# Prompt attention on one Trainium2 core: a third bank for the transposes, a factor chain in two parts, and low halves subtracted on VectorE

## The chip, the cores and the metric

The program runs on one core of a Trainium2 chip, as one launch. The metric is the device time in microseconds of that core. The kernel before took 2014.07 us in the median of three runs (2012.44, 2014.07 and 2017.64). The engines are TensorE (PE for its matmuls, PEld for its weight loads), VectorE (DVE), ScalarE (ACT), GpSimd (POOL) and SyncE (SP, which issues most DMAs). Each engine works through its own queue in order.

## The reference, cut to what matters

One inference step of a two-layer decoder trunk, for a prompt of 1024 tokens and for 8 samples of 8 tokens. Layer 0 is a gated short convolution beside a memory cross-attention. Layer 1 is a latent attention with 8 heads beside a memory cross-attention. The change touches the prompt's latent attention in layer 1:

```python
q  = (rms_norm(cq, q_lora_g) @ w_uq).reshape(b, t, 8, 192)   # 128 plain + 64 rotary per head
qn = rms_norm(q, q_g)                                        # a factor per row and head
k_nope = einsum('btc,chd->bthd', ckv, w_uk)
kscale = rsqrt((sum(k_nope**2) + sum(kpe_raw**2)) / 192 + EPS)   # a factor per key and head
s = (q_abs . ckv + q_pe . kpe) * kscale * 192**-0.5          # causal, rows of 128 queries
p = softmax(s);  o_lat = p @ ckv
y_mla = einsum('bthc,chd->bthd', o_lat, w_uv)
out = concat(y_mla, y_mem) * silu(z);  y = x + out @ w_out
```

The kernel computes keys, queries and values per head from the latent (k = ckv w_uk, v = ckv w_uv), so that s = q k and y = p v directly.

## The kernel before, in words

All matrix products are made of fp32 numbers split into a high half (fp32r) and a low half (the rest), and are three matmuls each: high by high, low by high, high by low (helper `mm3`, lines 188 to 191). A split is two instructions: the high half is a copy that rounds, the low half a subtraction (helpers `sub`, line 179, and `split`, lines 181 to 186). Most rows of the profile that say L179 or L183 are such a subtraction or copy; the names of the tiles tell which. Weights come through the class `Stream`, which loads a tile, and splits it with the engines named in its arguments `le` (the low half; `"g"` is GpSimd, `"v"` VectorE) and `he` (the high half).

The program runs a long first part (both layers' projections and the samples' attention), then the preparation of the prompt's attention (`mla_pre`), then `mla()`, which is the eight heads, and then `out1()`, the last projection. In `mla()`, head h is worked on while head h+1 is prepared:

- `prep(h)` is a generator. It makes the head's keys (tiles `akH`, `akL`) and queries (`aqH`, `aqL`) with matmuls into the PSUM banks called `mm` (three of them), and the squares `asq`; then the sums of squares through the bank `v` (`ast`), and from these the factors 1/sqrt in a chain of small VectorE instructions on 128x16 numbers (`akv`, `aks`, `rsq`: lines 1376 to 1378, and `rsqrt_`, lines 202 to 206). The factors are transposed (`tk`), copied (`akt`), written to DRAM and read back as a row over all partitions (`akb`), which the scores need. Each `yield` gives way to the head that is being worked on.
- `vals(h)` makes the values of two heads at once (`avH`, `avL`), in even heads, in the steps i = 2 to 5.
- For each of eight blocks of 128 queries (i = 0 to 7): `soft` makes the scores (matmuls L1421 to L1427 into `mm` banks), multiplies them by `akb` and takes the maximum on VectorE (L1429, tile `ass`), makes the bias `anb` (L1432) and the exponentials on ScalarE (L1434), then the reciprocal `als`, and `scale` multiplies by it on ScalarE (L1441; i = 0 on VectorE). Two blocks later `step` follows: `tr` transposes the probabilities 128x128 by 128x128 into PSUM banks (`atp`, L1453), up to four to a bank; `trs` splits the bank into `aPTH` (ScalarE) and `aPTL` (VectorE); for every second i, `pvl` multiplies by the values into `aO` and VectorE multiplies by the gate (`as`, L1480).

In `prep` and `vals`, the lines `psplit(...)` split a bank of keys, queries or values. With `"g"` ScalarE copies the bank to `araw` in SBUF (L1320), GpSimd rounds it to the high half (L1321) and subtracts (L179); the bank is free after ScalarE. With `"v"` ScalarE writes the high half from the bank (L1324) and VectorE subtracts from the bank (L179, or L1328 for the queries, which carry a factor). Head 0 uses `"v"` for all; for the others the strings `PSP` (keys, queries) and `VSP` (the four parts of the values) decide. `O_ENG` names the engines for the last projection's weights (`who`, `wlo`).

The order of the instructions on each engine is set when the program is built: a scheduler takes the instructions of the generators and places each by its estimate of when it can start. PSUM has eight banks here: three `mm`, two with the tag `s` (where the transposes go), and one each with the tags `v`, `t` and `x`; `x` isn't used in `mla()`.

Of the kernel before, what the change touches and what calls it, by code (L numbers as in the profile page):

```python
# [5 lines left out]
F = mybir.dt.float32  # L6
R = mybir.dt.float32r
I32 = mybir.dt.int32
# [4 lines left out]
ALU = mybir.AluOpType  # L13
# [38 lines left out]
M_ENG = ("vvgv", "a")  # L52
A_ENG = ("v", "a")
SCL = "vaaaaaaa"
PSP = "ggg"
W_ENG = ("v", "a")
PT_ENG = "a"
NY = 7.0
MRB = 2
WQ = 1024  # L60
VSP = "vggg"
VI = (2, 3, 4, 5)
SLAG = 1
O_ENG = ("g", "a")
YG = ()
YORD = [(0, 2)] + [(b, x) for b in (11, 0, 1, 2, 3, 4, 5, 6, 7) for x in range(2)]
YLB = 6
# [25 lines left out]
def build(nc, tc, I, O):  # L93
    A, V, G, T, S = nc.scalar, nc.vector, nc.gpsimd, nc.tensor, nc.sync
# [38 lines left out]
    def mmt(name="mm"):  # L133
        return psm.tile([128, 512], F, tag="mm", name=name)

    def pst(tag, name):
        return psx.tile([128, 512], F, tag=tag, name=name, bufs=2 if tag == "s" else 1)
# [55 lines left out]
    cnt = [0]  # L193
    sm = {}

    def rsqrt_(p, out, v, shape):

        cnt[0] += 1
        t = p.tile(shape, F, tag="rsq", name=f"rsq{cnt[0]}")
        P = shape[0]  # L200
        t, out, v = t[0:P], out, v
        V.tensor_scalar(out=out.bitcast(I32), in0=v.bitcast(I32), scalar1=-0.5, scalar2=float(0x5F3759DF), op0=ALU.mult, op1=ALU.add)
        for _ in range(3):
            V.tensor_tensor(out=t, in0=out, in1=out, op=ALU.mult)
            V.scalar_tensor_tensor(out=t, in0=t, scalar=-0.5, in1=v, op0=ALU.mult, op1=ALU.mult)
            V.scalar_tensor_tensor(out=out, in0=t, scalar=1.5, in1=out, op0=ALU.add, op1=ALU.mult)

    def stat_r(p, sqs, tiles, n, tag, eps=EPS, keep=None):

        nt = len(tiles)  # L210
        ps = pst("x", "stat" + tag)
        for i, (c0, m) in enumerate(tiles):
            for j, sq in enumerate(sqs):
                T.matmul(ps[0:m, 2 * i:2 * i + 2], sq[:, c0:c0 + m], ones[:, 0:2], start=(j == 0), stop=(j == len(sqs) - 1))
        v = (keep or p).tile([128, nt], F, name="stv" + tag, tag="stv" + (tag if keep else ""))
        r = (keep or p).tile([128, nt], F, name="str" + tag, tag="str" + (tag if keep else ""))
        if tiles[-1][1] < 128:
            V.memset(v, 1.0)
        for i0, i1, m in ([(0, nt, 128)] if tiles[-1][1] == 128 else [(0, nt - 1, 128), (nt - 1, nt, tiles[-1][1])]):
            V.tensor_scalar(out=v[0:m, i0:i1], in0=ps[0:m, 2 * i0:2 * i1].rearrange("p (i two) -> p i two", two=2)[:, :, 0], scalar1=1.0 / n, scalar2=eps, op0=ALU.mult, op1=ALU.add)  # L220
        rsqrt_(p, r, v, [128, nt])
        return v, r
# [1009 lines left out]
    def mla_pre():  # L1232
# [12 lines left out]
        V.memset(fac[:, 0:8], 1.0 / 192)  # L1245
        V.scalar_tensor_tensor(out=fac[:, 8:16], in0=rcq[:, 0:8], scalar=1.0 / 192, in1=rcq[:, 0:8], op0=ALU.mult, op1=ALU.mult)
        pw = P.new("mw_")
        wq = Stream(pw, pw, [I["wuqn"][h] for h in range(8)], 384, "q", bufs=1)
        pw2 = P.new("mw2_")
        wk = Stream(pw2, pw2, [I["wuk"][h] for h in range(8)], 256, "k", bufs=1)  # L1250
        pw3 = P.new("mw3_")
        wv = Stream(pw3, pw3, [I["wuv"][h] for h in range(4)], 512, "v", bufs=1)
        wk.load_to(0)
        wq.load_to(0)
        wv.load_to(0)
# [11 lines left out]
        p = tp_.new("mt2")  # L1267
# [8 lines left out]
        p = tp_.new("mt3")  # L1276
        for i in range(8):
            ps = mmt()
# [16 lines left out]
            if i in CKI[0:2]:  # L1295
                k = CKI.index(i)
# [12 lines left out]
    def mla():  # L1309
        yield "X"  # L1310
        P, cqH, cqL, ckH, ckL, kpH, kpL, ssq, fac, wq, wk, wv = sm["mla"]
        LP = Pools()
        p = LP.new("ma_")
# [3 lines left out]
        def psplit(le, h, l, ps, scale=1.0):  # L1317
            if le == "g":
                t = p.tile([128, 512], F, name="araw", tag="araw", bufs=3)
                A.activation(t, ps, AF.Copy, scale=scale)  # L1320
                G.tensor_copy(h, t)  # L1321
                sub(G, l, t, h)
            else:
                A.activation(h, ps, AF.Copy, scale=scale)  # L1324
                if isinstance(scale, float):
                    sub(V, l, ps, h)
                else:
                    V.scalar_tensor_tensor(out=l, in0=ps, scalar=scale, in1=h.bitcast(F), op0=ALU.mult, op1=ALU.subtract)  # L1328

        def prep(h):  # L1330
# [7 lines left out]
            qp = p.tile([128, NP], R, name="aqp", tag=f"aqp{h % 2}")  # L1338
            qr = p.tile([128, NP], F, name="aqr", tag="aqr")
            S.dma_start(out=qr[0:64], in_=d_qp[h // 2, 64 * (h % 2):64 * (h % 2) + 64, :])  # L1340
            yield 0.5
            for c in range(2):
                ps = mmt()
                fm(ps, 512, w, 2, ckH, ckL, c * 512)
                sq = p.tile([128, 512], F, name="asq", tag="asq", bufs=4)
                A.activation(sq, ps, AF.Square)
                psplit("v" if h == 0 else PSP[0], kH[:, c * 512:(c + 1) * 512], kL[:, c * 512:(c + 1) * 512], ps)
                sqs.append(sq)
                if c == 0:
                    w2 = wq.get(h)  # L1350
                q = slice(c * 512, (c + 1) * 512)
# [4 lines left out]
            for c in range(2):  # L1356
                ps = mmt()
                fm(ps, 512, w, 3, cqH, cqL, c * 512)
                sq = p.tile([128, 512], F, name="asq", tag="asq", bufs=4)
                A.activation(sq, ps, AF.Square)  # L1360
                psplit("v" if h == 0 else PSP[1], qH[:, c * 512:(c + 1) * 512], qL[:, c * 512:(c + 1) * 512], ps, gq)
                sqs.append(sq)
# [11 lines left out]
            v = p.tile([128, 16], F, name="akv", tag="akv")  # L1374
            rs = p.tile([128, 16], F, name="aks", tag="aks")
            V.tensor_tensor(out=v.rearrange("p (j c) -> p j c", j=4), in0=st, in1=ssq[:, :, h].rearrange("p (j c) -> p j c", j=4), op=ALU.add)
            V.tensor_tensor(out=v, in0=v, in1=fac, op=ALU.mult)
            V.tensor_scalar(out=v, in0=v, scalar1=EPS, scalar2=None, op0=ALU.add)
            rsqrt_(p, rs, v, [128, 16])
            yield 1.0  # L1380
            tk = pst("v", "tk")
            T.transpose(tk[0:8, 0:128], rs[:, 0:8], ident)
            kt = p.tile([8, 128], F, name="akt", tag="akt")
# [58 lines left out]
            else:  # L1442
                V.tensor_scalar(out=ss[:, 0:kv], in0=ss[:, 0:kv], scalar1=ls, scalar2=None, op0=ALU.mult)

        PTs = {}

        def tr(i, ss):
            out = []
            for b0 in range(0, i + 1, 4):
                nb = min(4, i + 1 - b0)  # L1450
                ps = pst("s", "atp")
                for b in range(nb):
                    T.transpose(ps[:, b * 128:(b + 1) * 128], ss[:, (b0 + b) * 128:(b0 + b + 1) * 128], ident)  # L1453
                out.append((b0, nb, ps))
            return out
# [13 lines left out]
        def pvl(h, i, H, L):  # L1469
# [15 lines left out]
            end()  # L1485

        g0 = prep(0)
        for _ in range(5):
            next(g0)
# [14 lines left out]
        def step(h, i, ss):  # L1504
            t = tr(i, ss)
            flush()
            trs(h, i, t)
# [69 lines left out]
    def out1_pre():  # L1577
# [3 lines left out]
        pw = PR.new("o1w")  # L1581
        ws = Stream(pw, pw, [I["wo1"][u] for u in range(8)], 1536, "o1", *O_ENG, rbufs=1)
        ws.load_to(0)
# [239 lines left out]
    def chain(*gens):  # L1823
        for g in gens:
            yield from g

    fr = chain(group_a(GA, I["xA"]), ["P"], samp_prep(), ["S"], samp_attn(), samp_y(), ["Y", "pre"], mla_pre(), ["X"])
    fl = chain(mem_kv(), group_b(GB, I["xB"]), mla(), out1())
    interleave(fl, fr, RAT)
    S.dma_start(out=O["newc"], in_=newc)  # L1830
# [121 lines left out]
```

## Time and profile before

| | |
|---|---|
| median of three runs | 2014.07 us (2012.44 to 2017.64) |
| the profiled execution | 2021.16 us, of which the span of the trace is 2019.4 us |
| TensorE matmuls busy | 1918.3 us, 95% of the span |
| VectorE busy | 983.4 us, 49% |
| ScalarE busy | 744.7 us, 37% |
| GpSimd busy | 474.6 us, 24% |

The profiled execution is 7 us longer than the median of the runs. The page's shares are means over the whole program; the eight heads lie between 1560 and 1884 us, `out1()` behind them. In a row of the timeline, the number in square brackets is the time for which the engine sat idle before the instruction, and the name behind it what ended that.

### The profile page before, as it was taken

The numbers are of one execution on the slowest core, as the hardware profiler recorded it, in microseconds if no ns is written. First come the engines' busy times: TensorE is split into PE (matmuls) and PEld (weight loads), VectorE is DVE, ScalarE is ACT, GpSimd is POOL, SyncE is SP. The second block draws the span as 40 slices with busy tenths as digits, with TensorE's granted clock in tenths as the row PEclk, the third lists the DMA queues.
The fourth block names the chain that finished last, engine by engine and source line by source line (L and its number), as shares of the span: only waits on it lengthen the run. The fifth ranks groups of instructions, "written<-read, shape, count | busy, mean of one in ns | idle before, by whom it ended". The sixth has DMA issues, their size and how long they took to land. (4 is left out here: it accounts for less than half of the span.)

```text
span 2019.4 us, 35704 instructions
## 1 busy us (share of the span) xinstructions
PE 1918.3 (95%) x12508; PEld 1653.9 (82%) x12508; DVE 983.4 (49%) x2673; ACT 744.7 (37%) x1499; POOL 474.6 (24%) x493
## 2 busy tenths in 40 slices
PE   6998999999999999999999999999998899998999
PEld 5997998999997877777787766777787787787999
DVE  7659535456544434434322543444446656656300
ACT  6445223334311233323222422333333666666300
POOL 1200000000000233323433324333332443432120
PEclk8999999999999999999999989999999999999999
DMA  5563535433544688678997879877852211213532
GB/s 202 193 207 124 165 131 194 145 117 114 181 160 140 194 266 270 221 249 281 321 314 260 292 235 301 255 240 231 284 156 67 84 58 56 67 40 129 183 95 72
DMA packets 192884, 368.28 MB, mean 182 GB/s; under 512 B 27809, under 2 KB 135585, under 8 KB 191426
## 3 DMA queue, kind: packets, MB, share of 16 engines
q1 hardware_dynamic: 172178, 298.75, 45.5%
q0 software_dynamic: 20528, 67.26, 10.3%
q8 instruction: 99, 1.62, 0.3%
q14 instruction: 79, 0.65, 0.1%
HBM read 331.22 MB, written 34.70 MB: 181 GB/s over the span
## 5 line engine op out<-in xcount | busy, mean ns | idle before, releaser
L1078 POOL DMA_INDIRECT nat<-nat,IX x256 | 270.6, 1057 | 517.9 <-PE pv L1163 451.6
L189 PE MATMUL mm<-xH,whi 128*128 128x384 f32 (+1 forms) x1112 | 369.1, 332 | 6.5 <-ACT whi L183 6.5
L191 PE MATMUL mm<-xH,wli 128*128 128x384 f32 (+1 forms) x1112 | 364.0, 328 | 1.8 <-DVE wli L179 1.8
L190 PE MATMUL mm<-xL,whi 128*128 128x384 f32 (+1 forms) x1112 | 364.0, 327 | 0.0
L189 PEld LDWEIGHTS mm<-xH,whi 128*128 128x128 f32 x1112 | 211.6, 190 | 22.5 <-issue 10.0
L183 ACT ACTIVATE whi<-wri 128x1024 fp32r<-128x1024 f32 (+1 forms) x130 | 126.4, 979 | 278.2 <-PE mm L190 228.4
L190 PEld LDWEIGHTS mm<-xL,whi 128*128 128x128 f32 x1112 | 211.4, 190 | 3.0 <-issue 2.8
L191 PEld LDWEIGHTS mm<-xH,wli 128*128 128x128 f32 x1112 | 211.1, 190 | 3.3 <-DVE wli L179 2.6
L179 DVE TENSOR_TENSOR wli<-wri,whi 128x1024 fp32r<-128x1024 f32 (+1 forms) x130 | 147.0, 1136 | 123.9 <-ACT whi L183 122.6
L1163 PE MATMUL pv<-nat,PT 128*64 128x256 f32 x1024 | 141.0, 397 | 16.6 <-ACT PT L1143 13.8
L1092 PE MATMUL sAB<-rec,qar 128*64 128x256 f32 x1024 | 150.4, 389 | 1.9 <-DVE mx L1107 1.6
L1163 PEld LDWEIGHTS pv<-nat,PT 128*64 128x64 f32 x1024 | 76.6, 140 | 60.6 <-ACT PT L1143 21.3
L1092 PEld LDWEIGHTS sAB<-rec,qar 128*64 128x64 f32 x1024 | 79.4, 138 | 45.5 <-issue 12.8
L1107 DVE CUSTOM_DVE_ANT_1 ss<-sAB,rec,mx 128x256 f32<-128x256 f32 x120 | 57.9, 483 | 113.3 <-PE sAB L1097 68.8
L189 PE MATMUL mm<-nH,whi 128*128 128x384 f32 x304 | 104.8, 345 | 1.1 <-ACT mP L497 1.0
L190 PE MATMUL mm<-nL,whi 128*128 128x384 f32 x304 | 102.7, 338 | 0.1
L191 PE MATMUL mm<-nH,wli 128*128 128x384 f32 x304 | 102.2, 336 | 0.0
L189 PE MATMUL mm<-yHo,who 128*128 128x384 f32 (+1 forms) x288 | 96.9, 337 | 1.3 <-ACT yHo L183 1.3
L191 PE MATMUL mm<-yHo,wlo 128*128 128x384 f32 (+1 forms) x288 | 94.2, 327 | 0.0
L190 PE MATMUL mm<-yLo,who 128*128 128x384 f32 (+1 forms) x288 | 93.9, 326 | 0.0
L183 ACT ACTIVATE who<-wro 128x768 fp32r<-128x768 f32 (+3 forms) x44 | 38.1, 873 | 146.7 <-PE mm L190 115.5
L1434 ACT ACTIVATE ass<-ass,anb,arq 128x128 f32<-128x128 f32 (+3 forms) x64 | 55.4, 866 | 63.6 <-DVE anb L1432 63.6
(588 smaller groups left out, 4196.3 us busy)
## 6 DMA issues: line engine op xcount, KB each, us to landing
rec<-rec SPq DMA_DIRECT2D x512, 192.0 KB
wri<-wi SPq DMA_DIRECT2D x114, 512.0 KB
wro<-wo SPq DMA_DIRECT2D x29, 384.0 KB
smkv<-ckm SPq DMA_DIRECT2D x16, 512.0 KB
smkv<-cvm SPq DMA_DIRECT2D x16, 512.0 KB
wrm<-memw SPq DMA_DIRECT2D x7, 1024.0 KB
wro<-wo SPq DMA_DIRECT2D x7, 768.0 KB
yld<-d_ys SPq DMA_DIRECT2D x8, 544.0 KB
```

The costliest lines, as they stand in the source:

```text
L179: eng.tensor_tensor(out=out, in0=a, in1=h.bitcast(F), op=ALU.subtract)
L183: A.activation(h, src, AF.Copy)
L189: T.matmul(out, wh, xh, start=first, stop=False)
L190: T.matmul(out, wh, xl, start=False, stop=False)
L191: T.matmul(out, wl, xh, start=False, stop=last)
L1078: G.indirect_dma_start(out=t[:, j % 2, :], out_offset=None, in_=I["nat"], in_offset=bass.IndirectOffsetOnAxis(ap=IX[:, q:q + 1], axis=0), ...
L1092: T.matmul(s[x][64 * ab:64 * ab + 64, 0:256], QA[:, cb, b, :], part(t, cb * 128 + ab * 64)[:, 4 * x:4 * x + 4, :], start=(cb == 0), stop=F ...
L1107: V.tensor_tensor_reduce(out=ss[:, 256 * x:256 * x + 256].rearrange("p (g k) -> p g k", g=4), in0=s[x][:, 0:256].rearrange("p (g k) -> p g ...
L1163: T.matmul(d["v"][64 * ab:64 * ab + 64, 0:256], PT[:, j, ab, :], n[j][:, ab * 256:ab * 256 + 256], start=(i == 0 and j == 0), stop=(i == C ...
L1434: A.activation(ss[:, 0:kv], ss[:, 0:kv], AF.Exp, bias=nb, scale=d["rq"][:, i:i + 1], accum_out=ls)
```

## The change

```diff
--- before.py
+++ after.py
@@ -52,16 +52,16 @@
 M_ENG = ("vvgv", "a")
 A_ENG = ("v", "a")
 SCL = "vaaaaaaa"
-PSP = "ggg"
+PSP = "vvv"
 W_ENG = ("v", "a")
 PT_ENG = "a"
 NY = 7.0
 MRB = 2
 WQ = 1024
-VSP = "vggg"
+VSP = "vvvv"
 VI = (2, 3, 4, 5)
 SLAG = 1
-O_ENG = ("g", "a")
+O_ENG = ("v", "a")
 YG = ()
 YORD = [(0, 2)] + [(b, x) for b in (11, 0, 1, 2, 3, 4, 5, 6, 7) for x in range(2)]
 YLB = 6
@@ -204,6 +204,18 @@
             V.tensor_tensor(out=t, in0=out, in1=out, op=ALU.mult)
             V.scalar_tensor_tensor(out=t, in0=t, scalar=-0.5, in1=v, op0=ALU.mult, op1=ALU.mult)
             V.scalar_tensor_tensor(out=out, in0=t, scalar=1.5, in1=out, op0=ALU.add, op1=ALU.mult)
+
+    def rsqrt_steps(p, out, v, shape):
+
+        cnt[0] += 1
+        t = p.tile(shape, F, tag="rsq", name=f"rsq{cnt[0]}")
+        V.tensor_scalar(out=out.bitcast(I32), in0=v.bitcast(I32), scalar1=-0.5, scalar2=float(0x5F3759DF), op0=ALU.mult, op1=ALU.add)
+        for n in range(3):
+            V.tensor_tensor(out=t, in0=out, in1=out, op=ALU.mult)
+            V.scalar_tensor_tensor(out=t, in0=t, scalar=-0.5, in1=v, op0=ALU.mult, op1=ALU.mult)
+            V.scalar_tensor_tensor(out=out, in0=t, scalar=1.5, in1=out, op0=ALU.add, op1=ALU.mult)
+            if n != 1:
+                yield
 
     def stat_r(p, sqs, tiles, n, tag, eps=EPS, keep=None):
 
@@ -1245,11 +1257,11 @@
         V.memset(fac[:, 0:8], 1.0 / 192)
         V.scalar_tensor_tensor(out=fac[:, 8:16], in0=rcq[:, 0:8], scalar=1.0 / 192, in1=rcq[:, 0:8], op0=ALU.mult, op1=ALU.mult)
         pw = P.new("mw_")
-        wq = Stream(pw, pw, [I["wuqn"][h] for h in range(8)], 384, "q", bufs=1)
+        wq = Stream(pw, pw, [I["wuqn"][h] for h in range(8)], 384, "q", "v", bufs=1)
         pw2 = P.new("mw2_")
-        wk = Stream(pw2, pw2, [I["wuk"][h] for h in range(8)], 256, "k", bufs=1)
+        wk = Stream(pw2, pw2, [I["wuk"][h] for h in range(8)], 256, "k", "v", bufs=1)
         pw3 = P.new("mw3_")
-        wv = Stream(pw3, pw3, [I["wuv"][h] for h in range(4)], 512, "v", bufs=1)
+        wv = Stream(pw3, pw3, [I["wuv"][h] for h in range(4)], 512, "v", "v", bufs=1)
         wk.load_to(0)
         wq.load_to(0)
         wv.load_to(0)
@@ -1338,7 +1350,6 @@
             qp = p.tile([128, NP], R, name="aqp", tag=f"aqp{h % 2}")
             qr = p.tile([128, NP], F, name="aqr", tag="aqr")
             S.dma_start(out=qr[0:64], in_=d_qp[h // 2, 64 * (h % 2):64 * (h % 2) + 64, :])
-            yield 0.5
             for c in range(2):
                 ps = mmt()
                 fm(ps, 512, w, 2, ckH, ckL, c * 512)
@@ -1376,8 +1387,8 @@
             V.tensor_tensor(out=v.rearrange("p (j c) -> p j c", j=4), in0=st, in1=ssq[:, :, h].rearrange("p (j c) -> p j c", j=4), op=ALU.add)
             V.tensor_tensor(out=v, in0=v, in1=fac, op=ALU.mult)
             V.tensor_scalar(out=v, in0=v, scalar1=EPS, scalar2=None, op0=ALU.add)
-            rsqrt_(p, rs, v, [128, 16])
-            yield 1.0
+            for _ in rsqrt_steps(p, rs, v, [128, 16]):
+                yield 0.5
             tk = pst("v", "tk")
             T.transpose(tk[0:8, 0:128], rs[:, 0:8], ident)
             kt = p.tile([8, 128], F, name="akt", tag="akt")
@@ -1442,13 +1453,14 @@
             else:
                 V.tensor_scalar(out=ss[:, 0:kv], in0=ss[:, 0:kv], scalar1=ls, scalar2=None, op0=ALU.mult)
 
-        PTs = {}
+        PTs, ntr = {}, [0]
 
         def tr(i, ss):
             out = []
             for b0 in range(0, i + 1, 4):
                 nb = min(4, i + 1 - b0)
-                ps = pst("s", "atp")
+                ps = pst("ssx"[ntr[0] % 3], "atp")
+                ntr[0] += 1
                 for b in range(nb):
                     T.transpose(ps[:, b * 128:(b + 1) * 128], ss[:, (b0 + b) * 128:(b0 + b + 1) * 128], ident)
                 out.append((b0, nb, ps))
```

In the eight heads the low halves of keys, queries and values, and those of the weights of all three and of the last projection, are subtracted on VectorE; the high halves are written by ScalarE straight from the bank. GpSimd keeps the rotary half of the queries (`aqp`, two instructions a head) and small copies. The transposes go round three banks (s, s, x). The `yield` ahead of the keys is gone, so that everything in `prep` comes one step earlier, and the chain of factors is cut in two by a `yield` behind its first round.

The instructions of GpSimd that go leave it with this in the heads: two `aqp` for each head. On VectorE and TensorE the order changes as follows; line numbers of the changed kernel are 12 higher from line 217 on (L1429 becomes L1440, L1453 becomes L1465, and the chain's L202 to L206 become L212 to L216).

VectorE, where the head turns: block 0 of a head (`ass` 128x128) and what follows it, before:

```order
L1429 ISA ass,amx<-mm,akb 128x128
L1429 ISA amx 128x1
L1432 SCALAR_TENSOR_TENSOR anb<-amx,arq 128x1
L1435 RECIPROCAL als<-als 128x1
L1443 TENSOR_SCALAR ass<-ass,als 128x128
L1480 SCALAR_TENSOR_TENSOR as_21609<-as_21609,aO 128x256
L179 TENSOR_TENSOR aPTL<-atp,aPTH 128x4x128
L179 TENSOR_TENSOR aPTL<-atp,aPTH 128x3x128
L1429 ISA ass,amx<-mm,akb 128x256
L1429 ISA amx 128x1
```

and after the change, with the keys of the next head (`akL`) and a weight (`wlk`) in the same place:

```order
L1440 ISA ass,amx<-mm,akb 128x128
L1440 ISA amx 128x1
L1443 SCALAR_TENSOR_TENSOR anb<-amx,arq 128x1
L179 TENSOR_TENSOR akL<-mm,akH 128x512
L1446 RECIPROCAL als<-als 128x1
L1454 TENSOR_SCALAR ass<-ass,als 128x128
L179 TENSOR_TENSOR akL<-mm,akH 128x512
L179 TENSOR_TENSOR wlk<-wrk,whk 128x256
L1492 SCALAR_TENSOR_TENSOR as_21593<-as_21593,aO 128x256
L179 TENSOR_TENSOR aPTL<-atp,aPTH 128x4x128
L179 TENSOR_TENSOR aPTL<-atp,aPTH 128x3x128
L1440 ISA ass,amx<-mm,akb 128x256
```

The two subtractions of keys stand ahead of the `aPTL` of block 6 (the 4x128 and the 3x128).

VectorE, blocks 5 and 6 of a head, where the chain of factors (L204 to L206 on `rsq` and `aks`) meets the `aPTL` of block 3 (128x4x128), before:

```order
L205 SCALAR_TENSOR_TENSOR rsq_22046<-rsq_22046,akv 128x16
L206 SCALAR_TENSOR_TENSOR aks<-rsq_22046,aks 128x16
L204 TENSOR_TENSOR rsq_22046<-aks 128x16
L205 SCALAR_TENSOR_TENSOR rsq_22046<-rsq_22046,akv 128x16
L1429 ISA ass,amx<-mm,akb 128x512
L1429 ISA amx 128x1
L206 SCALAR_TENSOR_TENSOR aks<-rsq_22046,aks 128x16
L179 TENSOR_TENSOR aPTL<-atp,aPTH 128x4x128
L204 TENSOR_TENSOR rsq_22046<-aks 128x16
L1429 ISA ass,amx<-mm,akb,amx 128x384
L1429 ISA amx 128x1
```

and the same `aPTL` after the change, where the chain (L214 to L216) has ended ahead of it:

```order
L1443 SCALAR_TENSOR_TENSOR anb<-amx,arq 128x1
L216 SCALAR_TENSOR_TENSOR aks<-rsq_21958,aks 128x16
L214 TENSOR_TENSOR rsq_21958<-aks 128x16
L215 SCALAR_TENSOR_TENSOR rsq_21958<-rsq_21958,akv 128x16
L216 SCALAR_TENSOR_TENSOR aks<-rsq_21958,aks 128x16
L1401 SCALAR_TENSOR_TENSOR arq<-aks,rcq 128x8
L1446 RECIPROCAL als<-als 128x1
L179 TENSOR_TENSOR avL<-mm,avH 128x512
L179 TENSOR_TENSOR aPTL<-atp,aPTH 128x4x128
L1440 ISA ass,amx<-mm,akb 128x512
L1440 ISA amx 128x1
L1395 COPY akt<-tk 8x128
```

The chain begins a block of scores earlier than before; in a head with values, `avL` and `wlv` stand in between, and `anb` of block 6 behind `wlv`.

TensorE in the same head, from the transposes of block 3 (`atp` x4), before:

```order
L1453 MATMUL atp<-ident,ass 128x128 x4
L189 MATMUL aO<-aPTH,avH 128x256
L1421 MATMUL mm<-akH,aqH 128x512
L1453 MATMUL atp<-ident,ass 128x128
L190 MATMUL aO<-aPTL,avH 128x256
L191 MATMUL aO<-aPTH,avL 128x256
L189 MATMUL aO<-aPTH,avH 128x256
L190 MATMUL aO<-aPTL,avH 128x256
L191 MATMUL aO<-aPTH,avL 128x256
L189 MATMUL aO<-aPTH,avH 128x256
L1382 MATMUL tk<-ident,aks 8x128
```

and after:

```order
L1436 MATMUL mm<-kpL,aqp 128x384
L1438 LDWEIGHTS idb
L1438 MATMUL mm<-cmb,idb 128x128
L1393 MATMUL tk<-ident,aks 8x128
L1465 MATMUL atp<-ident,ass 128x128 x5
L189 MATMUL aO<-aPTH,avH 128x256
L190 MATMUL aO<-aPTL,avH 128x256
L191 MATMUL aO<-aPTH,avL 128x256
L189 MATMUL aO<-aPTH,avH 128x256
L190 MATMUL aO<-aPTL,avH 128x256
```

The transpose of the factors (`tk`) stands ahead of all transposes of block 4, which are now in one row, and no longer among the products `aO`.

## Rows read from the trace of the kernel before

**Rows 1.** Windows by stage: length, busy us (instructions) by engine, PE clock, DMA share, GB/s.

```profile
1560.00:1602.00 42.00, 38.03 (x207) 29.11 (x206) 22.60 (x68) 24.49 (x51) 17.36 (x17) 0.92 0.32 92
1602.00:1830.00 228.00, 212.05 (x1390) 179.35 (x1389) 136.19 (x447) 149.99 (x298) 92.08 (x94) 0.99 0.20 62
1830.00:1884.00 54.00, 49.50 (x317) 44.30 (x316) 35.43 (x91) 38.24 (x61) 5.85 (x6) 0.94 0.50 168
```

**Rows 2.** Waits of PE, 1602 to 1830 us: total us, times, longest.

```profile
PE atp L1453 <- DVE rsq L204: 9.9, 6, 3.0
PE atp L1453 <- DVE aPTL L179: 5.0, 6, 0.8
PE aO L189 <- ACT aPTH L183: 0.7, 3, 0.2
PE tk L1382 <- DVE aks L206: 0.3, 1, 0.3
```

**Rows 3.** Timeline, 1673 to 1678 us: start, duration, engine, line, tile, idle before.

```profile
1673.30 1.31 POOL L179 TENSOR_TENSOR avL<-araw,avH 128x512 fp32r<-128x512 f32 x1
1673.50 1.15 DVE L206 SCALAR_TENSOR_TENSOR aks<-rsq,aks 128x16 f32<-128x16 f32 x1
1674.58 1.27 POOL L179 TENSOR_TENSOR wlv<-wrv,whv 128x512 fp32r<-128x512 f32 x1
1674.68 1.20 DVE L204 TENSOR_TENSOR rsq<-aks 128x16 f32<-128x16 f32 x1
...
1676.70 0.68 DVE L179 TENSOR_TENSOR aPTL<-atp,aPTH 128x512 fp32r<-128x512 f32 x1
...
1677.53 0.45 PE L1453 MATMUL atp<-ident,ass 128*128 128x128 f32 x1 [2.37 <-DVE rsq L204]
```

**Rows 4.** Timeline of head 1, which makes no values, 1634 to 1645 us.

```profile
1634.50 0.17 DVE L206 SCALAR_TENSOR_TENSOR aks<-rsq,aks 128x16 f32<-128x16 f32 x1
...
1636.53 0.30 PE L1453 MATMUL atp<-ident,ass 128*128 128x128 f32 x1 [0.71 <-DVE rsq L204]
...
1644.55 0.55 PE L1453 MATMUL atp<-ident,ass 128*128 128x128 f32 x3 [0.84 <-DVE aPTL L179]
```

**Rows 5.** Windows of 8 us with a low clock; columns as in rows 1.

```profile
1572.00:1580.00 8.00, 4.84 (x22) 4.01 (x21) 5.02 (x10) 1.95 (x5) 3.51 (x3) 0.67 0.27 68
...
1676.00:1684.00 8.00, 6.47 (x36) 5.89 (x37) 5.90 (x22) 4.21 (x8) 0.52 (x1) 0.79 0.33 102
...
1828.00:1836.00 8.00, 6.23 (x33) 5.38 (x33) 5.82 (x21) 4.67 (x8) 2.01 (x3) 0.79 0.39 128
```

**Rows 6.** Groups on DVE: line, tile, form, count | busy us, mean ns | idle before.

```profile
L1432 DVE SCALAR_TENSOR_TENSOR anb<-amx,arq 128x1 f32<-128x1 f32 x64 | 21.0, 329 | 1.2
...
L179 DVE TENSOR_TENSOR avL<-mm,avH 128x512 fp32r<-128x512 f32 x7 | 4.8, 687 | 0.4 <-ACT avH L1324 0.3
...
L1328 DVE SCALAR_TENSOR_TENSOR aqL<-mm,gq,aqH 128x512 fp32r<-128x512 f32 x2 | 1.5, 751 | 2.8 <-ACT aqH L1324 2.8
...
L179 DVE TENSOR_TENSOR wli<-wri,whi 128x256 fp32r<-128x256 f32 x16 | 6.3, 424 | 2.4 <-ACT whi L183 2.0 <-issue 0.4
```

**Rows 7.** Group on POOL that stays, 1560 to 1884 us.

```profile
L179 POOL TENSOR_TENSOR aqp<-aqr,aqp 64x512 fp32r<-64x512 f32 x16 | 20.3, 1284 | 66.0 <-issue 60.8 <-ACT aqp L1352 5.0
```

**Rows 8.** A bank held by VectorE in head 0 (timeline); VectorE's longest wait, all heads.

```profile
1567.62 0.19 PEld L189 LDWEIGHTS mm<-whv,ckH 128*128 128x128 f32 x1 [0.84 <-DVE aqL L1328]
...
DVE als L1435 <- ACT ass L1434: 37.3, 46, 1.2
```

**Rows 9.** Timeline of head 0: the factors' transpose, and the first scores.

```profile
1576.39 0.37 PE L1382 MATMUL tk<-ident,aks 128*8 128x128 f32 x1 [2.99 <-DVE aks L206]
...
1583.28 0.29 DVE L1429 CUSTOM_DVE_ANT_0 ass<-mm,akb 128x128 f32<-128x128 f32 x1 [6.12 <-DMA akb<-d_ks]
```

**Rows 10.** Timeline of head 7: a load for the last projection, and PE behind it.

```profile
1854.50 1.11 ACT L183 ACTIVATE yHp<-yr 128x1088 fp32r<-128x1088 f32 x1 [2.87 <-DMA yr<-d_ym]
...
1857.89 1.39 PE L1453 MATMUL atp<-ident,ass 128*128 128x128 f32 x5 [2.33 <-DVE aPTL L179]
```

## The prediction

> **What bounds the kernel now.** I read the stages first, then TensorE's waits in the stage that the change touches, then the instructions around the longest waits, and last VectorE's groups there. In the windows by stage [rows 1] the reader is to see that TensorE is nearly the whole of the eight heads: in heads 1 to 6 it is busy for 212.05 of 228.00 us while VectorE is for 136.19, ScalarE for 149.99 and GpSimd for 92.08. So only TensorE's idle time can be won, and what its clock loses: 228.00 − 212.05 = 15.95 us in heads 1 to 6, 3.97 in head 0 (with the start) and 4.50 in head 7 and the step into the last projection, 24.4 in all. The clock column gives (1 − 0.92) × 42 + (1 − 0.99) × 228 + (1 − 0.94) × 54 = 3.4 + 2.3 + 3.2 = 8.9 us of full-speed time lost. The two together, 33 us, are the most that this change can save there.
>
> TensorE's waits [rows 2] are the 15.9 us of heads 1 to 6, and nearly all of it is the transposes `atp` waiting for VectorE. They wait for a bank. The six waits of 0.8 us on `aPTL` are the bank itself [rows 4]. The 9.9 us put down to the factor chain are the same thing: the transpose of block 4's last part stops until the `aPTL` of block 3 has emptied one of the two banks, and that `aPTL` stands in VectorE's queue in the middle of the chain. The trace shows it: `aPTL` runs from 1676.70 for 0.68 us, and TensorE starts again at 1677.53 after 2.37 us [rows 3]. These waits are short, 0.71 us, in heads without values [rows 4] and 2.4 to 3.0 us in heads with values. The difference is GpSimd: an instruction of the chain that takes 0.17 us by itself [rows 4] takes 1.15 us beside GpSimd's `avL` and 1.20 us beside its `wlv`, and ends when they end [rows 3].
>
> **The change part by part.** *Third bank and earlier chain.* With banks s, s, x, a transposition reuses a bank three allocations later instead of two, so that block 4's last part needs the bank of block 2, whose `aPTL` is done well before. The six waits of 0.8 us and the six on the chain's `aPTL` lose their cause: −9.9 − 5.0 − 0.3 (`tk`) = −15.2 us. What is late next: the products `aO` of blocks 2 and 3 need the `aPTL` of block 3, and this now stands behind the end of the chain and, with values, behind an `avL`. The rows show such a wait only as 0.7 us in three heads [rows 2]; at worst all of `avL` and `aPTL`, 0.69 + 0.68 = 1.4 us [rows 6, 3], is waited for in each of the six heads, 8 us. In heads with values TensorE has 12 matmuls of values and ten scores ahead of it. I take 0.5 us a head, nearer to the row that there is: +3. Six heads: 15.95 − 3 = −13 us.
>
> *GpSimd's subtractions.* On VectorE come, per the groups' durations [rows 6]: 14 `akL` and 9 `avL` at 0.687 us, 14 `aqL` at 0.751, and the weights. Between 256 and 512 columns a subtraction grows by (687 − 424)/256 = 1.03 ns a column, so 7 `wlk` at 0.424, 7 `wlq` (384 columns) at 0.556, 3 `wlv` at 0.687, and in head 7 four pieces of `wlo` at 0.556 and one of 1536 columns at 1.74: 15.8 + 10.5 + 3.0 + 3.9 + 2.1 + 4.0 = 39.3 us in the heads. What goes on VectorE is the stretching: 64 `anb` take 329 ns on the mean [rows 6] where an instruction as small takes 0.17 [rows 4], 64 × 0.16 = 10 us, and two instructions of the chain lose 1 us each in each of three heads with values, 6 us. GpSimd was busy for 17.36 + 92.08 + 5.85 = 115.3 us [rows 1] and keeps 20.3 [rows 7], so some 82% of the 16 us go, 13. VectorE's busy time in the heads rises from 194.2 us [rows 1] to about 220, from 60% to about 72% of a stage of some 305 us. In the turn of a head, where the new subtractions of keys and queries stand, VectorE was waiting anyway: its 37.3 us behind ScalarE's exponentials alone [rows 8] are as long as all that is added. So I cost the work itself at nothing while this cover lasts.
>
> The Trainium skill weighs against that: "Perfetto Trace Analysis", Optimizing Scalar/DVE Operations, says that work may be moved to ScalarE or even GpSimd when VectorE is saturated, and that moves between VectorE and GpSimd may bring nothing, since they share a read port of SBUF. The trace shows the sharing [rows 3], and a VectorE far from saturated [rows 1]; by the page's first half the sum would be that of the second rival below.
>
> *Banks of the projections.* A bank of keys, queries or values is now free after VectorE's subtraction and no longer after ScalarE's copy. There are 37 such. In head 0, which was made so already, the nearest row is one stall of 0.84 us on TensorE's weight loads [rows 8], and none of its matmuls waited. So between 0 and 37 × 0.84 = 31 us; I take 0, since eleven of head 0's twelve such banks show nothing, and keep the other end for the range.
>
> *Clock.* At 1676 and 1828 us the clock falls behind the gaps of 2.4 and 3.0 us: (1 − 0.79) × 8 = 1.7 us each [rows 5]. Without gaps of this length it should not: −3.
>
> *Head 0.* The factors' transpose waits 2.99 us for the chain [rows 9], and the clock loses 0.33 × 8 = 2.6 [rows 5]. The chain starts 12 matmuls sooner and `wlv` no longer blocks it, but `aqp` still does, and the first scores need the factors' way through DRAM, 6.1 us of waiting on VectorE [rows 9], with little else for TensorE. I take −2, from −4 to +1.
>
> *Head 7.* Its 2.33 us of TensorE come after a wait of ScalarE for a load [rows 10], which stays. VectorE gets the 4.0 us of `wlo` among the scores, and there is no next head to fill gaps. Between −3 and +4 (all of `wlo` waited for); I take 0.
>
> *The rest.* The first pieces of the weights, 12 subtractions of 64 to 128 columns, move to VectorE ahead of the heads; they stand before its busiest stretch there, where TensorE's shares hide them: 0 to +1. In the last projection VectorE has 16 us of work in 135, and six `wlo` of 1.74 us, each behind the adds that free the banks, cost nothing.
>
> Sum: −13 − 3 − 2 + 0 = −18 us. The profiled execution would go from 2021.2 to 2003 us, and the median, which lies 7.1 us lower, from 2014.1 to **1996 us**.
>
> **The rivals.** (1) *The banks become the wait.* Three `mm` banks are held longer, and in the long blocks VectorE comes late to each. At a third of head 0's stall, 37 × 0.3 = 11 us are given back: 2007 us. For it: each score needs two banks from block 4 on. Against it: TensorE has 12 to 24 matmuls of `aO` or values between a bank's end and its next use.
>
> (2) *VectorE becomes the bound in the long blocks.* Between the scores of blocks 5 and 6 VectorE must now do the chain, `avL`, `aPTL`, `wlv` and a maximum, and each time waits for the exponentials, 37.3/46 = 0.8 us [rows 8]. If its queue there is longer than TensorE's work, each of the blocks 4 to 7 costs TensorE a stall of about 1 us (that wait and a part of an `avL`), in seven heads 4 × 7 × 1.0 = 28 us, against 18 saved: 2024 us, slower than before. It decides from the point where VectorE's share in the second half of a head passes 90%; the mean of 72% and the place of the new work in the first half speak against it.
>
> (3) *The change doesn't free VectorE.* If the stretching is `aqp`'s as much as the others', the chain still meets it: two instructions of 1 us in six heads, 12 us of the gain, 2008 us. Against it: both long instructions stand beside `avL` and `wlv` [rows 3].
>
> **How the numbers follow.** 0.3% of the median, 6 us, is about what a measurement of this kernel can tell from no change. My forecast gets 0.66, with a range of its own from 1986 (clock and head 7 come out well) to 2006; rival 1 gets 0.17, rival 3 0.06, rival 2 0.11 with everything else that makes it slower by 6 us. Rivals 1 and 3 lie at the border of 2008 and go half to "faster", half to "same"; some of the forecast's upper tail goes to "same" too. So faster 0.75, same 0.15, slower 0.10. The floor of the range is 1981 if all 33 us went; I cut at 1984, and above at 2012, which takes in rivals 1 and 3 and leaves out rival 2.
>
> **What would show it right or wrong.** Right: no wait of `atp` on `aPTL` or the chain over 0.3 us in heads 1 to 6; TensorE idle there for 2 to 5 us instead of 15.95; `anb` at 160 to 200 ns on the mean; the chain's instructions at 0.17 us; VectorE busy for about 220 us in the heads; no low clock at the places of the former gaps. Wrong: new waits of the `mm` matmuls on `akL`, `aqL` or `avL` of several us in all (rival 1), or VectorE over 90% busy in the blocks 4 to 7 with TensorE waiting for maxima and `aPTL` (rival 2), or chain instructions of over 1 us beside `aqp` (rival 3). If head 7 shows more than 4 us more idle time, the weights of the last projection were mis-sized.

## The result, and the profile after

The changed kernel took 1991.94 us (median of 8 runs, 1986.88 to 2002.43) and the kernel before 2013.26 us (8 runs, 2009.00 to 2029.57). The ratio is 0.9891, 95% interval [0.9858, 0.9923]: 21.9 us saved, where 18 were forecast and 1996 us predicted. Its profiled execution took 1989.2 us with a span of 1987.4, 32.0 less than the profiled one of before. Of these 32 us, 4.8 lie ahead of the heads, where the forecast had none and no cause was sought, 27.1 in the heads and 0.1 behind them.

The eight heads are taken here, in every kernel, from the end of the last transpose `qpt` to the first product with `yLf`: TensorE does the same work between these two. The window of before, then that of the changed kernel (columns as in [rows 1]):

```profile
1558.67:1877.83 319.16, 294.75 (x1877) 247.67 (x1876) 188.81 (x601) 208.75 (x407) 115.29 (x117) 0.97 0.25 78
```

```profile
1553.86:1845.94 292.08, 284.41 (x1877) 242.63 (x1876) 206.84 (x660) 206.96 (x407) 22.03 (x21) 1.00 0.28 86
```

TensorE's idle time (length less busy time) fell from 24.4 to 7.7 us, and its busy time for the same work from 294.75 to 284.41. The two are the 27.1 us. Of the 10.3 us of busy time some 8.5 are the clock's (0.97 before and 1.00 after; the falls are counted below). VectorE is busy for 206.84 us, 71% of the stage. TensorE's waits after, in the heads:

```profile
PE atp L1465 <- DVE aPTL L179: 3.0, 5, 1.6
PE tk L1393 <- DVE aks L216: 2.3, 1, 2.3
PE mm L190 <- DVE yLf L179: 1.2, 1, 1.2
PE atp L1465 <- ACT ass L1452: 0.3, 1, 0.3
PE mm L189 <- DVE akL L179: 0.2, 1, 0.2
```

Of the twelve waits of [rows 2] on the chain and on `aPTL` there remain two of 0.4 us, in heads 2 and 4. Of the rest of the first line 0.5 us is head 7's, and 1.8 lie at the end of head 6, among the first low halves of the last projection's weights, where the kernel before had no wait:

```profile
1807.79 0.41 PE L1465 MATMUL atp<-ident,ass 128*128 128x128 f32 x2 [1.57 <-DVE aPTL L179]
```

What answers to the stretched chain of [rows 3], in the same head 2, by the timeline (rows of other work left out):

```profile
1657.26 0.17 DVE L214 TENSOR_TENSOR rsq<-aks 128x16 f32<-128x16 f32 x1
...
1660.41 0.17 DVE L216 SCALAR_TENSOR_TENSOR aks<-rsq,aks 128x16 f32<-128x16 f32 x1
...
1661.53 0.69 DVE L179 TENSOR_TENSOR avL<-mm,avH 128x512 fp32r<-128x512 f32 x1 [0.32 <-ACT avH L1336]
...
1662.14 0.68 DVE L179 TENSOR_TENSOR aPTL<-atp,aPTH 128x512 fp32r<-128x512 f32 x1
1662.19 0.27 PE L1393 MATMUL tk<-ident,aks 128*8 128x128 f32 x1
1662.30 0.71 PE L1465 MATMUL atp<-ident,ass 128*128 128x128 f32 x5
```

The chain is done at 1660.6, the factors' transpose comes 1.6 us later and waits for nothing, and the five transposes of block 4 don't wait for the `aPTL` beside them.

### The profile page after: what moved, and what is told of

Read it like the earlier page. It is cut to its first block, busy times and chain, and to the rows that moved or that the text cites. A ratio compares the mean times of both kernels' runs of the same rounds, so it can differ in the third digit from the quotient of the medians.

```text
span 1987.4 us, 35607 instructions
## 1 busy us (share of the span) xinstructions
PE 1900.8 (96%) x12508; PEld 1644.0 (83%) x12508; DVE 1013.6 (51%) x2750; ACT 742.9 (37%) x1499; POOL 353.9 (18%) x379
## 4 chain that ended last, share of the span: by engine, by line
PE 70%; issue 13%; DVE 6%; DMA 3%; POOL 3%; ACT 3%; another core or an unknown queue 0%; SPq 0%; POOLq 0%; DVEq 0%; ACTq 0%
PE mm L189 16%; PE mm L190 16%; PE mm L191 16%; PE pv L1175 4%; PE sAB L1104 4%; POOL nat L1090 3%; PE sAB L1109 1%; PE atp L1465 1%; PE ptp L1148 1%; PE aO L190 1%; PE aO L191 1%; PE aO L189 1%; DVE ass L1440 1%; PE mm L1432 1%; DMA wnr<-wi1n 1%
```

## The experiments

The experiments ran on three chips, on which the kernel before had medians of 1997.42, 2011.33 and 2012.42 us, so ratios are compared, and stages within the profiles. The table has the ratio; the length of the eight heads and TensorE's idle time there (the window's length less its busy time); and how many of VectorE's small instructions (128 x 1, 8 or 16) took over 0.3 us there, with the time that they took beyond 0.17 us each, counted in the timelines.

| kernel | ratio, 95% interval | heads, us | PE idle, us | stretched |
|---|---|---|---|---|
| before | 1 | 319.2 | 24.4 | 28, 20.2 us |
| changed | 0.9891 [0.9858, 0.9923] | 292.1 | 7.7 | 8, 6.0 us |
| changed, once more | 0.9889 [0.9859, 0.9920] | 293.7 | 7.7 | 8, 6.1 us |
| third bank alone | 0.9968 [0.9952, 0.9985] | 310.4 | 18.2 | 33, 20.5 us |
| both edits of the chain | 0.9911 [0.9890, 0.9931] | 300.8 | 13.7 | 30, 15.2 us |
| - earlier preparation alone | 0.9959 [0.9938, 0.9979] | 302.7 | 15.3 | 29, 17.3 us |
| - chain in two parts alone | 1.0039 [1.0016, 1.0062] | 322.8 | 27.1 | 34, 21.6 us |
| low halves on VectorE alone | 0.9933 [0.9915, 0.9951] | 305.4 | 16.6 | 7, 5.8 us |
| changed, two banks | 0.9891 [0.9872, 0.9911] | 293.7 | 8.7 | 8, 6.0 us |
| changed, `wlo` on GpSimd | 0.9902 [0.9886, 0.9919] | 292.9 | 7.8 | 9, 6.9 us |
| changed, `wlk` `wlq` `wlv` on GpSimd | 0.9881 [0.9863, 0.9899] | 292.6 | 6.4 | 12, 7.1 us |
| changed, keys, queries, values on GpSimd | 0.9894 [0.9874, 0.9913] | 294.8 | 8.2 | 21, 10.1 us |
| changed, `aqp` on VectorE | 0.9898 [0.9877, 0.9919] | 293.3 | 7.6 | 0 |
| weights on GpSimd, `aqp` on VectorE | 0.9895 [0.9865, 0.9924] | 292.6 | 7.4 | 5, 2.4 us |

**One part at a time, on the kernel before.** *The third bank:*

```
-                ps = pst("s", "atp")
+                ps = pst("ssx"[ntr[0] % 3], "atp")
+                ntr[0] += 1
```

> The kernel before with the third bank for the transposes alone; factor chain and GpSimd's subtractions as before. Theory A (two causes in a row: the bank, and behind it the chain): the six waits of 0.84 us on aPTL go, and so does the bank's part of the six waits put down to the chain, but the transpose of the factors (tk) stands a few instructions behind and now waits for the chain's end itself, some 2 us in each of the three heads with values. Saved: 5.0 + 3 x 0.7 + 1 = 8 us, ratio about 0.996, and the clock still falls behind two of the gaps. Theory B (the bank alone is the cause, the rest of the change is not needed): all 15.2 us of waits go and 3 us of clock, ratio about 0.991, as with the whole change.

Measured 0.9968, 6.4 us, near theory A; B is out. But the wait didn't go where A said. TensorE's first waits in the heads, and head 2 by the timeline:

```profile
PE aO L190 <- DVE aPTL L179: 9.4, 7, 2.5
PE tk L1382 <- DVE aks L206: 3.4, 3, 2.6
```

```profile
1651.53 1.15 DVE L206 SCALAR_TENSOR_TENSOR aks<-rsq,aks 128x16 f32<-128x16 f32 x1
...
1652.72 1.19 DVE L204 TENSOR_TENSOR rsq<-aks 128x16 f32<-128x16 f32 x1
...
1654.73 0.68 DVE L179 TENSOR_TENSOR aPTL<-atp,aPTH 128x512 fp32r<-128x512 f32 x1
...
1655.47 0.38 PE L190 MATMUL aO<-aPTL,avH 128*128 128x256 f32 x1 [2.40 <-DVE aPTL L179]
```

The transposes run on, and the product that needs the same `aPTL` waits for it, 2.40 us where the transpose had waited 2.37 [rows 3]. The bank removed the waits of 0.84 us and little else: 5.0 of the 6.2 us by which TensorE's idle time fell.

*Both edits of the chain:*

```
-            yield 0.5
...
-            rsqrt_(p, rs, v, [128, 16])
-            yield 1.0
+            for _ in rsqrt_steps(p, rs, v, [128, 16]):
+                yield 0.5
```

> The kernel before with the factor chain in two parts and the preparation one step earlier alone; two banks, GpSimd's subtractions as before. Theory A: the six waits of 0.84 us stay (5 us); of the 9.9 us put down to the chain about 7 go, since most of the chain now runs a block earlier, and head 0 and the clock give some 3 us: 10 us saved, ratio about 0.995. The chain's small instructions still take over 1 us beside GpSimd. Theory B (the bank alone counts): nothing over 3 us, ratio 0.9985 or more.

Measured 0.9911, 17.8 us: much more than theory A gave it, and most of the whole change, with GpSimd still stretching 30 instructions. No wait is over 0.8 us from head 1 to head 5 (the longest, 1.2, stands at the end of head 6), and the 0.84 us waits are 0.6 or less:

```profile
PE atp L1464 <- DVE aPTL L179: 8.8, 13, 1.2
PE tk L1393 <- DVE aks L216: 2.3, 1, 2.3
```

*The two edits apart* (the `yield 0.5` alone, and `rsqrt_steps` alone):

> The kernel before with the preparation one step earlier alone (one yield taken out); chain in one part, two banks, GpSimd's subtractions as before. Theory G, from the run with both edits of the chain (ratio 0.9911): the earlier step is what puts the chain's end ahead of the bank that the transposes wait for, so this line alone gives as much: ratio 0.990 to 0.993, heads 2 to 7 some 13 us shorter than in the profile of before, no wait of atp over 0.8 us there. Theory H (the division of the chain is what does it): under 4 us, ratio 0.998 or more, waits of 2.4 us still there.

> The kernel before with the factor chain in two parts alone; preparation, banks and GpSimd's subtractions as before. Theory G: aPTL comes ahead of the chain's last six instructions and no more, and the chain still ends in the same block as its aPTL: the waits of 2.4 to 3.0 us fall to 1 to 2, those of 0.84 us stay, 2 to 6 us saved, ratio 0.997 to 0.999. Theory H: ratio about 0.991, as with both.

Neither G nor H holds. The earlier step gives 8.3 us, the division loses 7.9, and together they save 17.8. With the step alone the chain still ends in a block in which the factors' transpose stands right behind it; the waits on `aPTL` go but for two of 0.5 us and one of 2.0 in head 7, and TensorE waits for the chain itself, eight times:

```profile
PE tk L1381 <- DVE aks L206: 9.1, 8, 2.2
PE atp L1452 <- DVE aPTL L179: 3.1, 4, 2.0
```

```profile
1661.60 1.31 POOL L179 TENSOR_TENSOR avL<-araw,avH 128x512 fp32r<-128x512 f32 x1
1661.79 1.15 DVE L205 SCALAR_TENSOR_TENSOR rsq<-rsq,akv 128x16 f32<-128x16 f32 x1
...
1666.03 0.27 PE L1381 MATMUL tk<-ident,aks 128*8 128x128 f32 x1 [1.34 <-DVE aks L206]
```

The division puts the transpose a step later, which this needs. Without the earlier step it leaves the bank's wait as it was, and of the 2.7 us of idle time that it adds 1.9 are one new wait in head 7; by the profiles it is 3.6 us slower, and where the rest of the 7.9 is was not found:

```profile
PE atp L1465 <- DVE aPTL L179: 17.1, 15, 3.0
```

*The low halves on VectorE* (`PSP`, `VSP`, the three streams and `O_ENG`):

```
+PSP = "vvv"
+VSP = "vvvv"
+O_ENG = ("v", "a")
```

> The kernel before with all the low halves on VectorE alone (keys, queries, values, their weights, and those of the last projection); two banks, chain as before. Theory A (GpSimd stretches the chain): anb falls from 329 to about 200 ns, the three waits of 2.4 to 3.0 us fall to 0.7 or less, the clock no longer drops at 1676 and 1828 us, the 0.84 us waits stay: 6 + 3 = 9 us saved, ratio about 0.9955. Theory C (work on VectorE costs what the third bank and the split must hide): the new subtractions delay aPTL, the six waits of 0.84 us grow to over 1.5 us, ratio 1.000 or more.

Measured 0.9933, 13.4 us, above theory A's 9; C is out. The waits of 2.4 to 3.0 us are gone, those of 0.84 us are 0.8, and three of 0.9 to 1.0 us on the chain's end are new (`tk`, in heads without values):

```profile
PE atp L1453 <- DVE aPTL L179: 6.7, 8, 1.4
PE tk L1382 <- DVE aks L206: 4.9, 5, 1.7
```

The three parts alone save 6.4 + 17.8 + 13.4 = 37.6 us, all together 21.9: they remove the same idle time.

**One part undone, on the changed kernel.** *Two banks again:*

> The changed kernel with two banks for the transposes again; chain and VectorE's subtractions as changed. Theory A: the waits of the atp on aPTL come back, six of 0.8 us and six of up to 0.7, 5 to 9 us slower than the changed kernel, ratio to before about 0.993. Theory B (the bank alone is the cause): 15 us or more slower than the changed kernel, ratio about 0.997 to 0.999.

Both theories are wrong: nothing is lost. The transposes wait three times for 0.6 us, in heads 1, 3 and 5, and once for 2.3 us at the end of head 6, where the third bank has 1.57:

```profile
PE atp L1464 <- DVE aPTL L179: 4.0, 4, 2.3
```

*The low halves of the last projection's weights, of the other weights, and of keys, queries and values on GpSimd again:*

> The changed kernel with the low halves of the last projection's weights on GpSimd again (O_ENG). Theory A (they cost VectorE nothing that TensorE waits for, nor did they cost anything on GpSimd): ratio to before as that of the changed kernel, 0.989 within 0.002; the stage of head 7 within 1 us of the changed kernel's. Theory D (the gain of head 7, some 3 us more than forecast, is theirs, since GpSimd no longer stretches head 7's small instructions): head 7 is 2 to 4 us longer, ratio about 0.9905.

> The changed kernel with the low halves of wk, wq and wv on GpSimd again. Theory A (their GpSimd instructions, 1.27 us each for wlv, stretch the small instructions beside them, but the chain is now early enough to take that): under 3 us, ratio about 0.990. Theory E (a wlv beside the chain costs a wait again in each head with values): three waits of 1 to 2 us, 3 to 6 us slower than the changed kernel, ratio about 0.992.

> The changed kernel with the low halves of keys, queries and values of heads 1 to 7 on GpSimd again, behind a copy of the bank by ScalarE (PSP, VSP); weights, bank and chain as changed. Theory A (with the chain early and three banks, stretched instructions no longer reach TensorE): within 3 us of the changed kernel, ratio about 0.990. Theory F (GpSimd's 37 subtractions and 28 casts are what the stretching comes from, and it stands in each head's chain): anb back at over 300 ns, 6 us or more slower than the changed kernel, ratio 0.992 or more.

Theory A holds three times; D, E and F are out. In the last of the three GpSimd works for 93.61 us in the heads and 21 instructions are stretched, and TensorE is idle for 0.6 us more than in the changed kernel. `anb` is at 227 ns there, not over 300; with the weights on GpSimd too (both edits of the chain) it is at 314. In the second, with `wlk`, `wlq` and `wlv` on GpSimd, the two waits of 0.4 us are gone too:

```profile
PE atp L1465 <- DVE aPTL L179: 2.0, 2, 1.6
```

So they came from these low halves on VectorE, most likely from `wlv`, which runs in the changed kernel right ahead of an `anb` that ScalarE's exponentials need. This is 0.8 us of TensorE's time and can't be told in the ratio.

```profile
1664.08 0.68 DVE L179 TENSOR_TENSOR wlv<-wrv,whv 128x512 fp32r<-128x512 f32 x1
1664.68 0.14 DVE L1443 SCALAR_TENSOR_TENSOR anb<-amx,arq 128x1 f32<-128x1 f32 x1
```

**Further than the change.** *`aqp` on VectorE:*

```
-                sub(G, qp[64:128, q], qr[0:64, q], qp[0:64, q])
+                sub(V, qp[64:128, q], qr[0:64, q], qp[0:64, q])
```

> The changed kernel with the last of GpSimd's subtractions in the heads, the 16 of aqp, on VectorE as well. If what is left of the stretching comes from GpSimd, anb falls from 218 to 160 ns and the wait of head 0's factors (2.32 us, two instructions of 1.2 us beside aqp) falls below 1 us. Theory A: the 16 x 0.69 = 11 us of added VectorE work lie in its idle time; 1 to 3 us faster than the changed kernel, ratio about 0.988. Theory C (VectorE is close to being the bound): new waits on aPTL of 0.4 us or more in each head, slower than the changed kernel, ratio 0.991 or more.

> The changed kernel with the weights of keys, queries and values on GpSimd again and aqp on VectorE, the two variants that each left TensorE the fewest waits in one stage (0.56 us from head 2 to head 7 in the one, 0.62 us for head 0's factors in the other). If waits add up by stage: 2 us less than the changed kernel, which is at the limit of what can be told, ratio 0.987 to 0.989. If the wait goes elsewhere: ratio as the changed kernel, 0.989 to 0.990.

Not one small instruction is stretched any more, and head 0's factors are waited for 0.62 us instead of 2.32. `anb` in the changed kernel, then here:

```profile
L1443 DVE SCALAR_TENSOR_TENSOR anb<-amx,arq 128x1 f32<-128x1 f32 x64 | 13.9, 218 | 1.3
```

```profile
L1443 DVE SCALAR_TENSOR_TENSOR anb<-amx,arq 128x1 f32<-128x1 f32 x64 | 9.9, 155 | 1.3
```

Yet no time is won, so that theory A fails, and C is out. 1.7 us went at one place and came back behind it: `ast` now waits 0.7 us for ScalarE, and products wait for `aqL`, 0.8 us in all. The mixture of both variants ends at 0.9895. No version beats the changed kernel by what can be told.

*The changed kernel once more:*

> The changed kernel itself once more, beside the three above on one chip. Its ratio was 0.9891 with an interval of 0.9858 to 0.9923; it should be 0.988 to 0.991 here. Its stages tell how far two profiles of one kernel agree: heads 2 to 7 within 1 us of 174.2, what lies ahead of the heads within some 20 us, and whether the clock of 1.0 all through the heads is the rule or luck.

Its waits repeat to 0.1 us. Its clock doesn't: it fell once, in head 0, behind the same wait of 2.32 us that the first profile has too. The clock (third number from the end) has a mean of 0.79 in the last window: it stood at 1.2 GHz for a part of it and at 2.4 GHz for the rest. The windows of the first profile, and of this one:

```profile
1562.00:1570.00 8.00, 6.16 (x48) 5.63 (x47) 6.54 (x16) 2.71 (x5) 2.51 (x2) 1.00 0.42 110
1570.00:1578.00 8.00, 7.36 (x39) 5.32 (x40) 5.31 (x15) 4.50 (x9) 2.69 (x2) 1.00 0.48 149
```

```profile
1560.00:1568.00 8.00, 6.40 (x49) 5.63 (x47) 6.33 (x15) 2.83 (x6) 2.51 (x2) 1.00 0.41 110
1568.00:1576.00 8.00, 7.27 (x33) 5.72 (x34) 4.24 (x10) 4.49 (x9) 1.70 (x2) 0.79 0.40 132
```

## Why the prediction came out, step by step

The time and the sign were right; the cause that carried the largest term was not. That the number came out so well is in part luck: the bank got the credit for what the two edits costed together with it do, and the low halves, costed at nothing, save 13.4 us when they are alone.

- **Third bank and earlier chain (−13).** The size was right: TensorE's idle time in heads 1 to 6 went from 15.95 us to 3.3, within the 2 to 5 forecast (the first two numbers of the rows below, before and after, each up to the first `anb` of head 7). The step that failed is its claim that with three banks the waits "lose their cause". The third bank alone hands the wait to `aO`, as this step's own "what is late next" had it, but at the full 0.6 and 2.4 us and not 0.5; and without the bank the changed kernel is as fast (0.9891). The cause was the place of `aPTL` in the middle of the chain, and the two edits of the chain, costed together with the bank, do the larger part by themselves: 7.4 us of idle time are left in these heads (0.9911). The bank alone leaves 10.1, and so do VectorE's low halves alone, by which the chain is no longer stretched. The prediction read the wait to its end, found `aPTL` inside the chain, and then credited the edit nearest to the transposes.

```profile
1602.00:1838.80 236.80, 220.85 (x1442) 186.94 (x1440) 142.79 (x469) 157.18 (x310) 93.34 (x96) 0.99 0.22 66
```

```profile
1588.00:1812.50 224.50, 221.21 (x1482) 190.43 (x1481) 161.59 (x538) 159.44 (x317) 15.72 (x14) 1.00 0.23 73
```

- **GpSimd's subtractions (0 net, 13 of 16 us of stretching gone).** The work added to VectorE is 39.6 us by its groups (forecast 39.3); the stretched instructions fell from 28 to 8, from 20.2 to 6.0 us, 14.2 saved. VectorE's busy time rose by 18.0 us, from 188.81 to 206.84, and not by the 26 forecast: instructions in a row overlap in the trace (`avL` of 1661.53 runs to 1662.22, the `aPTL` behind it starts at 1662.14). Its share is 71% (forecast 72%), and only the two waits of 0.4 us come from it. What was mis-sized is the 0: stretched instructions of the chain stand ahead of the `aPTL` [rows 3], and with these subtractions on VectorE alone the kernel before is 13.4 us faster. Beside the two edits of the chain this gain is not added again. That `aqp` would keep its part is shown by the run that moved it: the last 6.0 us are its own. The mechanism that the prediction took from the trace, a small instruction that ends with GpSimd's, is shown by this run too. "SBUF — State Buffer", Who interferes with whom, in the Trainium skill, says that a VectorE instruction with two inputs in SBUF contends with a GpSimd instruction that reads SBUF, and that one with at most one such input does not outside certain modes. In the run with both edits of the chain the trace agrees: 28 `anb` and `rsq` with two inputs began beside a GpSimd subtraction and took 0.31 to 1.25 us, while twelve reciprocals (one input, as small as `anb`) began beside a subtraction or a cast of GpSimd and took at most 167 ns. But an instruction with one input is stretched in it too: `aks<-akv` takes 0.47 us instead of 0.17 beside GpSimd's cast, in three heads. Whether it ran in one of those modes no run shows.

```profile
L1446 DVE RECIPROCAL als<-als 128x1 f32<-128x1 f32 x64 | 10.4, 163 | 46.3 <-ACT ass L1445 45.8
```

```profile
1641.15 0.61 POOL L1333 CAST avH<-araw 128x512 fp32r<-128x512 f32 x1 [2.61 <-ACT araw L1332]
1641.33 0.47 DVE L212 TENSOR_SCALAR aks<-akv 128x16 int32<-128x16 int32 x1
```

- **Banks of the projections (0, end of range 31 us).** TensorE's matmuls wait once for `akL`, 0.16 us; its weight loads, from which the end of the range was taken, wait 2.0 us in all for `akL` and `aqL`. Right, and the rival built on it is out. Head 0 has eight such banks (two of keys, two of queries, four of values) and not twelve, which changes no term.
- **Clock (−3).** Right: the two falls at 1676 and 1828 us, 3.4 us, are gone in both profiles of the changed kernel. In all the kernel before loses some 8.5 us in the heads (the prediction's 8.9 come from rounded shares): 3.4 in head 0 [rows 1], these two, and one more behind the wait of 2.33 us in head 7, (1 − 0.79) × 8 = 1.7 us by the row below, which had not been counted. The changed kernel loses none in its first profile and 1.7 in its second.

```profile
1854.00:1862.00 8.00, 5.67 (x28) 4.87 (x27) 4.87 (x14) 5.51 (x8) 0.24 (x1) 0.79 0.32 100
```

- **Head 0 (−2, from −4 to +1).** The factors are waited for 2.32 us instead of 2.99 [rows 9], because `aqp` still stretches two instructions, as forecast; and the wait of `ast` (0.8) is gone. TensorE's idle time falls by 1.5 us. With the clock this is some −5 in the first profile, beyond the range's end, and −3 in the second, so the term hangs on the clock.
- **Head 7 (0, from −3 to +4).** The prediction held that the 2.33 us behind ScalarE's wait for a load stay. They don't: the load is there in time, and the same copy waits for nothing (row below). From its first `anb` on, TensorE's idle time fell from 4.50 to 1.9 us, and with 1.7 of clock this is some −4, beyond the range's end. The low halves of the last projection's weights don't bring it, for with them on GpSimd again the wait is not back; which edit does is not known.

```profile
1824.32 1.11 ACT L183 ACTIVATE yHp<-yr 128x1088 fp32r<-128x1088 f32 x1
```

- **The rivals.** VectorE as the bound: out, since in the second half of a head with values it is busy for 14.58 of 18.90 us, 77% and not over 90 (row below), and since 16 more subtractions there cost nothing. The chain still stretched by `aqp`: true in head 0 only, 2.3 us. The sum of the forecast's terms, 18 us, fell 3 us short of the medians' difference and 9 short of the heads' 27.1 us in the profiles; these started 7.9 us above the median of before and ended 2.7 below that of after, so that part of their difference is the two executions'.

```profile
1653.00:1671.90 18.90, 18.50 (x128) 16.51 (x128) 14.58 (x53) 12.65 (x24) 2.55 (x2) 1.00 0.23 72
```

- **The signs.** TensorE's idle time and the clock at the former gaps came out as said. The waits of `atp` did not stay under 0.3 us (0.4 twice, 1.57 at the end of head 6), and `anb` is at 218 ns and not at 160 to 200, by what `aqp` still does to it.

What stays open: whether the bank and VectorE's work add anything to the two edits of the chain. The profiles say so (13.7 us idle against 7.7), and that either will do (8.7 with VectorE's work and no bank, 8.2 with the bank and the keys, queries and values on GpSimd); the ratios, 0.9911 and 0.9891, have intervals that overlap. The two edits of the chain with the third bank, but without VectorE's work, were not run.

## What to carry to other kernels

When a wait names a bank, ask who else needs the instruction that frees it: another bank removed the waits of 0.84 us here, where nobody did, and only moved those where the very next product did. Where several edits aim at one wait, their gains don't add (37.6 us singly, 21.9 together), so an edit is judged by undoing it too, and one that loses alone can be what makes another pay. Stretched instructions are worth removing only where somebody waits at the end of them.

## What was not expected of the hardware

One and the same wait of TensorE, 2.32 us in head 0, was followed by a mean granted clock of 0.79 over the next 8 us in one execution of the changed kernel and of 1.00 in another; in the kernel before, the gap of 2.37 us at 1677 us cost clock [rows 5] and that of 2.42 us, which ended at 1754.05, did not, by the windows there:

```profile
1748.00:1756.00 8.00, 5.58 (x39) 4.84 (x38) 6.58 (x22) 4.15 (x9) 3.15 (x3) 1.00 0.03 10
1756.00:1764.00 8.00, 7.16 (x47) 5.79 (x47) 5.72 (x17) 7.24 (x14) 2.53 (x2) 1.00 0.49 133
```

So 2 us at such a place come and go between executions of one kernel, and two profiles can't settle a term of that size.
